# A hybrid attention layer: TensorE's order written out by hand through the attention, with the small steps spread over quarter granules

## The chip, the cores and the metric

One NeuronCore of a Trainium2 chip runs the whole layer. The metric is the device time of one execution in microseconds (us); the time before is the median of three runs.

## The reference, cut to what matters

One decoder layer for 512 tokens of width 2048, all in float32. Four heads of gated linear attention (GLA, in chunks) and four heads of differential softmax attention share one input projection; their outputs stand side by side and go through one output projection `w_o`.

```python
proj = h @ w_in                                   # 2048 -> 6160 columns
gq, gk, gv, gg, ga, dq, dk, dv = split(proj)
log_a = log_sigmoid(ga @ w_alpha_up + b_alpha) / 16
# GLA, per head (dk 128, dv 256):
#   o_t = q_t S_t,  S_t = diag(a_t) S_{t-1} + k_t^T v_t      (causal)
o_a = rmsnorm(gla(gq, gk, gv, log_a), gla_norm) * silu(gg)
# differential attention, per head and block of 128 queries:
#   p = softmax(q k^T * scale + alibi) for each of two halves;  a = p1 - lam * p2
o_b = rmsnorm(a @ dv, diff_norm) * (1 - lambda_init)
y = concat(o_a, o_b) @ w_o
```

Norms, the residual and a gated FFN with a short convolution follow; the change doesn't touch them.

## The kernel before, in words

**Products.** A float32 product is made of three TensorE matmuls on split numbers: high part times high part, and the two mixed ones. The left side stands in SBUF as `ah` and `al` (high and low parts of the activations, 16 slots of 128 features). The weights come in granules of 128x1024 (0.5 MB): SyncE (SP) issues a load into `raw` (4 buffers), ScalarE (ACT) writes the high part `whi` (L122), VectorE (DVE) the low part `wlo` (L123). A granule feeds 24 matmuls of 128x512, called products here.

**The attention stage.** From 395.86 us to about 670 us the kernel runs 31 granules (744 products): four each for `dq` and `dk` of diff head 3 (`stage_qk`, `proj_t`, `mm_t`, L158 to L160), eight for each of the two gate columns (`gate(0)`, `gate(1)`, `proj_n`, `mm_n`, L178 to L180), and the first seven of `w_o`'s first column. Everything before it made q, k, v and the decay sums of the heads and stored them in DRAM.

**The small work beside them.** Two generators hold the attention. `gla_chain` runs the four GLA heads one after the other: k·q (L745), seven levels of decayed scores (each four matmuls L736, with DVE and ACT work on the tiles `d` and `qe` and a masked copy into `sc`), then per head a serial tail: transposes of `kd` (L767), and for each of four chunks the output (L779, L780), its norm (ACT square, two POOL operations, DVE L784 into the SBUF tile `oa`), and the state (L787, DVE). `diff_chain` runs 16 blocks (4 heads, 4 query blocks): the scores of two halves (L813) with a softmax on DVE and ACT (L815 to L829, in `probs`), in the next step the transposes of the probabilities (L836, `turned`), in the one after the values (L844) with a norm, and last the transposes of the output (L855, `store`) to ACT and to DRAM (`dod`). `step()` runs once per granule and advances the two by GLA_PACE 2.0 and DIFF_PACE 0.7 steps.

**What sets the order.** The program only says which work belongs beside which granule. The Tile scheduler puts the instructions of each engine in order, TensorE's too, by a simulated time line; on the chip each engine then runs its list strictly in that order. PSUM has eight banks: four (`psm`) for the products' sums, four (`psa`) for all the small work, taken in turn. A tile with n buffers waits for the use n tiles back.

**The end of the stage.** `w_o` needs its left side in `ah` and `al`. The GLA part comes by `gla_rows` (load the gate `sg`, multiply `oa`, L929, transpose by L143 into slots 8 to 15), the diff part by `reload(h)` (load `dod` into `dr`, split into slots 2h and 2h+1). `FIRST` is the order of `w_o`'s granules; entry g takes slots 2g and 2g+1. Before, it begins with 4 and 5, the slots of GLA heads 0 and 1, which are ready only when their rows are transposed, in the middle of the small work; diff heads 0 and 1 (entries 0 and 1) follow.

Of the kernel before, what the change touches and what calls it, by code (L numbers as in the profile page):

```python
# [33 lines left out]
GLA_PACE, DIFF_PACE = 2.0, 0.7  # L34
# [3 lines left out]
def hybrid_layer(ctx: ExitStack, tc: tile.TileContext, x, attn_pre_norm, w_in, w_alpha_up, b_alpha,  # L38
# [10 lines left out]
    def dma(o, i):  # L49
        return nc.sync.dma_start(out=o, in_=i)  # L50

# [98 lines left out]
    def mm_t(banks, g, w, t0, t1, first=0, last=KT // 4 - 1):  # L150
# [12 lines left out]
    def proj_t(w3, col, emit, order=tuple(range(KT // 4))):  # L163
        banks = [bank(psm) for _ in range(2)]
        for g in order:
            w = granule(w3[:, 4 * g:4 * g + 4, col:col + 256], 4)
            mm_t(banks, g, w, 0, NT, order[0], order[-1])
            if g == order[-1]:
                for n in range(2):
                    emit(n, banks[n])  # L170
            step()
# [11 lines left out]
    def proj_n(w3, col, emit, order=tuple(range(KT)), first=0, banks=None, seq=tuple(range(KT // 2)), upto=KT // 2,  # L183
               after=None):
# [175 lines left out]
    dod = [dram.tile([P, 2, S], F32, name=f"dod{h}") for h in range(DH)]  # L360
    sgd = [dram.tile([P, NT, 512], F32, name=f"sgd{c}") for c in range(2)]
# [257 lines left out]
    def mix_unit(cols2, dsts, prods):  # L619
# [20 lines left out]
        def done(j):  # L640
            dma(dsts[j], st[j])
# [6 lines left out]
    units += [mix_unit((C_DQ + 256 * h, C_DK + 256 * h), (dqd[h], dkd[h]), up_prods) for h in range(STRASSEN_HEADS)]  # L648
# [40 lines left out]
    oa = [mc.tile([P, NT, 512], F32, name=f"oa{c}", bufs=1) for c in range(2)]  # L689
# [12 lines left out]
    SG = GDK ** -0.5  # L702

# [3 lines left out]
    def gla_head(h, q, k, b):  # L707
        bc = b.rearrange("p (c x) -> p c x", c=4)
        v = "p (n x) -> p n x"
        eb = mc.tile([P, S], F32, name="eb", tag="eb", bufs=1)  # L710
        sc = mc.tile([P, 4, P], F32, name="sc", tag="sc", bufs=1)
# [12 lines left out]
        def apply(hs, d):  # L724
# [4 lines left out]
            tt(d, d, k, ALU.mult)  # L729
# [20 lines left out]
        for li, hs in enumerate(LEVELS):  # L750
# [5 lines left out]
            if li + 2 == len(LEVELS):  # L756
                qb = tg("qb")
# [10 lines left out]
        kT = tg("kT")  # L768
        act(kT[:, :3 * P], kb[:, :3 * P], AF.Copy)
        yield  # L770
        vt = mc.tile([P, NT, GDV], F32, name="gv", tag="gv", bufs=1)
        dma(vt, gvd[h])
        g, e0 = h // 2, (h % 2) * GDV
        st = None
        for c in range(4):
# [8 lines left out]
            stt(oa[g][:, c, e0:e0 + GDV], po[:, :GDV], r, gnb, ALU.mult, ALU.mult)  # L784
# [9 lines left out]
            yield  # L794

# [67 lines left out]

    def gla_chain():
        nxt = gla_load(0)
        for h in range(GH):
            cur = nxt
            if h + 1 < GH:
                nxt = gla_load(h + 1)
            yield from gla_head(h, *cur)  # L870
            heads_done[0] = h + 1

    def diff_chain():
        todo = [(h, qb) for h in range(DH) for qb in range(NT)]
        held = [None] * 3
        while todo or any(held):
            for j, f in enumerate((store, values, turned)):
                if held[j]:
# [3 lines left out]
                    if j:  # L882
                        held[j - 1] = at, r
            if todo and todo[0][0] < heads_done[1]:
# [4 lines left out]
                if qb == NT - 1 and h + 1 < heads_done[1]:  # L889
# [3 lines left out]
    chains = [[gla_chain(), GLA_PACE, 0.0], [diff_chain(), DIFF_PACE, 0.0]]  # L893

    def both():
        while chains:
            for c in list(chains):
                c[2] += c[1]
                while c[2] >= 1.0:
                    c[2] -= 1.0  # L900
                    if next(c[0], 0) == 0:
                        chains.remove(c)
                        break
            yield

    def stage_qk(dsts, col, h, order=tuple(range(4))):
        def emit(n, b):
            t = mc.tile([P, S], F32, name="qs", tag="sg", bufs=2)
# [3 lines left out]
        proj_t(w_in3, col + 256 * h, emit, order)  # L912

    def gate(c):
        def emit(t, b):
            sg = mc.tile([P, S], F32, name="sg", tag="sg", bufs=2)
# [6 lines left out]
    def gla_rows(c, *ts):  # L923
        while heads_done[0] < 2 * c + 2:
            next(fill[0])
        for t in ts:
            sg = mc.tile([P, S], F32, name="sg", tag="sg", bufs=2)
# [12 lines left out]
    def reload(h):  # L940
        while heads_done[2] <= h:
            next(fill[0])
# [542 lines left out]
```

## Time and profile before

| | us |
|---|---|
| time, median of three runs | 2125.69 (2123.19 to 2129.04) |
| the profiled execution's own time | 2126.07 |
| its span in the profile | 2124.3 |
| TensorE busy in the span | 2074.1 (98%) |
| VectorE busy | 1559.1 (73%) |
| ScalarE busy | 960.4 (45%) |
| attention stage, 395.86 to 670 | 274.1, of which TensorE is busy 261.1 |

The profile tells for each engine when it was busy and, for each stretch of idle time, what ended it. TensorE's granted clock is given as a share of full speed: 1.00 is the upper of its two levels (2.4 GHz), a mean below it means that part of the stretch ran at the lower one (1.2 GHz).

### The profile page before, as it was taken

What the parts mean: (1) busy time and instruction counts of PE and PEld (TensorE: products, weight loads), DVE (VectorE), ACT (ScalarE), POOL (GpSimd) and SP (SyncE); (2) the same over time, 40 slices, a digit from 0 to 9 for tenths busy, and PEclk for the clock granted to TensorE, in tenths of its full rate; (3) what the DMA queues carried; (4) which work ended last, traced back from release to release, by engine and by line L of the source; (5) the groups of instructions that cost most, each with busy time, mean ns of one, the idle gap of its engine ahead of it and who ended that gap; (6) DMA issues with size and microseconds to landing.
All of it is one profiled execution on the core that took longest, in us unless ns stands there. A gap on an engine that the chain in (4) does not pass through costs nothing.

```text
span 2124.3 us, 34800 instructions
## 1 busy us (share of the span) xinstructions
PE 2074.1 (98%) x14161; PEld 1895.9 (89%) x14161; DVE 1559.1 (73%) x1873; ACT 960.4 (45%) x1217; POOL 245.4 (12%) x279
## 2 busy tenths in 40 slices
PE   7999999999989999999999999999999999999997
PEld 5899999888867888899999999999999888888886
DVE  7967667566785246788787786787878877988887
ACT  5435344345453234354544554544454554444433
POOL 1110111000011000011101111111111110110101
PEclk9999999999999999999999999999999999999999
DMA  7576675843425334465766757667577876776753
GB/s 263 140 173 168 152 179 134 287 127 126 134 83 186 99 129 169 129 139 129 171 168 159 175 135 192 149 157 192 132 171 174 249 215 176 181 198 156 182 155 139
DMA packets 251811, 349.10 MB, mean 164 GB/s; under 512 B 13744, under 2 KB 183140, under 8 KB 249860
## 3 DMA queue, kind: packets, MB, share of 16 engines
q1 hardware_dynamic: 181092, 265.09, 36.5%
q0 software_dynamic: 70560, 81.80, 24.6%
q8 instruction: 111, 1.82, 0.3%
q14 instruction: 48, 0.39, 0.1%
HBM read 301.23 MB, written 45.61 MB: 163 GB/s over the span
## 4 chain that ended last, share of the span: by engine, by line
PE 39%; issue 14%; DVE 3%; DMA 2%; POOL 1%; ACT 0%; POOLq 0%; DVEq 0%; SPq 0%; ACTq 0%
PE bank L316 11%; PE bank L315 11%; PE bank L314 11%; PE bank L160 1%; PE bank L159 1%; PE bank L158 1%; DVE wlo L123 1%; DMA raw<-in_w_ffn_out_dram 1%; POOL rt L228 1%; POOL raw L228 1%; PE bank L1266 1%; PE bank L1267 1%; DMA rt<-in_w_ffn_out_dram 0%; PE bank L1265 0%; PE bank L1390 0%
## 5 line engine op out<-in xcount | busy, mean ns | idle before, releaser
L122 ACT ACTIVATE whi<-raw 128x1024 fp32r<-128x1024 f32 x314 | 331.6, 1060 | 530.9 <-PE bank L315 164.1
L123 DVE TENSOR_TENSOR wlo<-raw,whi 128x1024 fp32r<-128x1024 f32 x314 | 381.6, 1221 | 242.9 <-ACT whi L122 236.7
L122 ACT ACTIVATE whi<-rt 128x1024 fp32r<-128x1024 f32 x306 | 322.8, 1060 | 357.3 <-PE bank L315 194.9
L123 DVE TENSOR_TENSOR wlo<-rt,whi 128x1024 fp32r<-128x1024 f32 x306 | 373.4, 1221 | 143.6 <-ACT whi L122 143.3
L314 PE MATMUL bank<-ah,whi 128*128 128x256 f32 x1600 | 442.3, 276 | 3.0 <-ACT gvs L528 2.1
L316 PE MATMUL bank<-ah,wlo 128*128 128x256 f32 x1600 | 442.4, 276 | 0.3 <-DVE wlo L123 0.2
L315 PE MATMUL bank<-al,whi 128*128 128x256 f32 x1600 | 442.0, 276 | 0.0
L314 PEld LDWEIGHTS bank<-ah,whi 128*128 128x128 f32 x1600 | 300.4, 188 | 3.9 <-ACT gvs L528 2.6
L316 PEld LDWEIGHTS bank<-ah,wlo 128*128 128x128 f32 x1600 | 300.3, 188 | 0.8 <-DVE wlo L123 0.7
L315 PEld LDWEIGHTS bank<-al,whi 128*128 128x128 f32 x1600 | 300.3, 188 | 0.1
L1266 PE MATMUL bank<-wlo,ah 128*128 128x512 f32 x560 | 219.0, 391 | 1.2 <-DVE wlo L123 1.2
L1267 PE MATMUL bank<-whi,al 128*128 128x512 f32 x560 | 218.5, 391 | 0.0
L1265 PE MATMUL bank<-whi,ah 128*128 128x512 f32 x560 | 213.6, 391 | 3.6 <-DVE acc L1273 1.9
L178 PE MATMUL bank<-whi,ah 128*128 128x512 f32 x448 | 177.6, 399 | 0.7 <-ACT ah L135 0.7
L179 PE MATMUL bank<-wlo,ah 128*128 128x512 f32 x448 | 177.6, 397 | 0.6 <-DVE wlo L123 0.6
L180 PE MATMUL bank<-whi,al 128*128 128x512 f32 x448 | 177.7, 400 | 0.0
L1265 PEld LDWEIGHTS bank<-whi,ah 128*128 128x128 f32 x560 | 105.2, 188 | 27.9 <-ACT whi L122 2.1
L1266 PEld LDWEIGHTS bank<-wlo,ah 128*128 128x128 f32 x560 | 105.5, 188 | 24.4 <-DVE wlo L123 2.5
L1267 PEld LDWEIGHTS bank<-whi,al 128*128 128x128 f32 x560 | 105.5, 188 | 21.9
L314 PE MATMUL bank<-s5h,whi 128*128 128x256 f32 x400 | 110.6, 276 | 1.0 <-ACT whi L122 1.0
L316 PE MATMUL bank<-s2h,wlo 128*128 128x256 f32 x400 | 110.8, 277 | 0.0
L316 PE MATMUL bank<-s5h,wlo 128*128 128x256 f32 x400 | 110.6, 276 | 0.0
(275 smaller groups left out, 4324.1 us busy)
## 6 DMA issues: line engine op xcount, KB each, us to landing
raw<-in_w_ffn_in_dram SPq DMA_DIRECT2D x96, 512.0 KB, 5.1
raw<-in_w_in_dram SPq DMA_DIRECT2D x64, 512.0 KB, 4.5
raw<-in_w_ffn_out_dram SPq DMA_DIRECT2D x48, 512.0 KB, 6.0
rt<-in_w_ffn_in_dram SPq DMA_DIRECT2D x40, 512.0 KB, 5.8
rt<-in_w_ffn_in_dram POOLq DMA_DIRECT2D x40, 512.0 KB, 5.9
raw<-in_w_ffn_in_dram POOLq DMA_DIRECT2D x40, 512.0 KB, 7.1
raw<-in_w_o_dram SPq DMA_DIRECT2D x32, 512.0 KB, 3.8
rt<-in_w_ffn_out_dram SPq DMA_DIRECT2D x20, 512.0 KB, 8.1
```

What stands on the lines that cost most here:

```text
L122: act(hi, raw, AF.Copy)
L123: tt(lo, raw, hi.bitcast(F32), ALU.subtract)
L178: mm(banks[t], ah[:, t, s, :], w[0][:, k, :], start=st, stop=False)
L179: mm(banks[t], ah[:, t, s, :], w[1][:, k, :], start=False, stop=False)
L180: mm(banks[t], al[:, t, s, :], w[0][:, k, :], start=False, stop=sp)
L228: nc.gpsimd.dma_start(out=raws[g].rearrange("p (a b) -> p a b", a=self.a), in_=self.block(0, j, g), accum_op=ALU.add)
L314: mm(o, wh, sh[:, :, kk, :], start=start and kk == 0 and n == 0, stop=False, **NOW)
L315: mm(o, wh, sl[:, :, kk, :], start=False, stop=False, **NOW)
L316: mm(o, wl, sh[:, :, kk, :], start=False, stop=kk == HK - 1, **NOW)
L1265: mm(b[j], sh[:, o:o + P], w[0][:, q, :], start=start and st == 0, stop=False, **NOW)
L1266: mm(b[j], sh[:, o:o + P], w[1][:, q, :], start=False, stop=False, **NOW)
L1267: mm(b[j], sl[:, o:o + P], w[0][:, q, :], start=False, stop=st == 3, **NOW)
```

## The change

- TensorE's order through the stage is the program's own (`manual_schedule` for that engine); the other engines are still ordered by the scheduler.
- `tick()` takes the place of `step()` there. It is called four times per granule, after every six products, and advances the GLA chain by 1.45/4 steps and the diff chain by 0.68/2 (a diff step now has two halves: store and values, then turned and scores). It also takes one entry of `turns`, the row work of `gla_rows`.
- `gla_head` ends after the levels; its serial tail is `gla_tail` and runs step by step beside the next head's levels. `eb` and `sc` have two buffers, `qb` and `kT` tiles of their own; `apply` multiplies only the first half of each pair in `d`, since the level reads no more.
- The GLA outputs no longer stay in `oa`: a tile `go` is stored to DRAM (`god`) from the POOL queue (`dma_aside`), and `gla_rows` loads it back into `ro` (two buffers) two rows ahead of its transposes.
- `gla_load(0)` and `diff_load(0)` stand ahead of the stage; the last two stores of diff head 2's q and k (`dqd`, `dkd`) go to the POOL queue.
- `FIRST` begins with 0, 1 (diff heads 0 and 1); `reload(0)` and `reload(1)` come after granules 5 and 6 of gate column 1, `gla_rows(0)` after its last, `gla_rows(1)` after `w_o`'s third. The order LATE moves from gate column 1 to gate column 0.

```diff
-GLA_PACE, DIFF_PACE = 2.0, 0.7
+GLA_PACE, DIFF_PACE = 1.45, 0.68
...
+    def dma_aside(o, i):
+        return nc.gpsimd.dma_start(out=o, in_=i)
...
+                if tick and k % 2:
+                    tick()
...
+                if tick:
+                    tick()
...
+    units += [mix_unit((C_DQ + 256 * h, C_DK + 256 * h), (dqd[h], dkd[h]), up_prods,
+                       dma_aside if h == STRASSEN_HEADS - 1 else dma) for h in range(STRASSEN_HEADS)]
...
-            tt(d, d, k, ALU.mult)
+            tt(dv[:, :, :hs], dv[:, :, :hs], k.rearrange(v, n=nb)[:, :, :hs], ALU.mult)
...
+        tails.append(gla_tail(h, kd, qb, eb, sc, vt))
+
+    def gla_tail(h, kd, qb, eb, sc, vt):
...
-            stt(oa[g][:, c, e0:e0 + GDV], po[:, :GDV], r, gnb, ALU.mult, ALU.mult)
+            go = mc.tile([P, GDV], F32, name="go", tag="go", bufs=2)
+            stt(go, po[:, :GDV], r, gnb, ALU.mult, ALU.mult)
+            dma_aside(god[h // 2][:, c, e0:e0 + GDV], go)
...
+    gla_in = {0: gla_load(0)}
+    diff_load(0)
+
     def gla_chain():
-        nxt = gla_load(0)
         for h in range(GH):
-            cur = nxt
             if h + 1 < GH:
-                nxt = gla_load(h + 1)
-            yield from gla_head(h, *cur)
-            heads_done[0] = h + 1
+                gla_in[h + 1] = gla_load(h + 1)
+            old = list(tails)
+            tails.clear()
+            for _ in gla_head(h, *gla_in[h]):
+                for g in old:
+                    next(g, None)
+                yield
+            for g in old:
+                for _ in g:
+                    yield
+        yield from tails[0]
...
+    chains = {"gla": [gla_chain(), GLA_PACE / 4, 0.0], "diff": [diff_chain(), DIFF_PACE / 2, -0.5]}
+
+    def advance(n):
+        if n in chains and next(chains[n][0], 0) == 0:
+            del chains[n]
+
+    def tick():
+        for n, c in list(chains.items()):
+            c[2] += c[1]
+            if c[2] >= 1.0:
+                c[2] -= 1.0
+                advance(n)
+        if turns:
+            turns.pop(0)()
+
+    turns = []
...
+    def gla_rows(c):
         while heads_done[0] < 2 * c + 2:
-            next(fill[0])
-        for t in ts:
-            sg = mc.tile([P, S], F32, name="sg", tag="sg", bufs=2)
+            advance("gla")
+        at = []
+
+        def fetch(t):
+            sg = mc.tile([P, S], F32, name="sg", tag="sg", bufs=3)
             dma(sg, sgd[c][:, t, :])
-            tt(oa[c][:, t, :], oa[c][:, t, :], sg, ALU.mult)
-            transpose_into_act(oa[c][:, t, :], t, 8 + 4 * c, 4)
-
-    fill.append(both())
-    pace[0], pace[1] = 1.0, 0.0
-    for h in range(STRASSEN_HEADS, DH):
-        late = (2, 3, 0, 1) if h == STRASSEN_HEADS else (0, 1, 2, 3)
-        stage_qk(dqd, C_DQ, h, late)
-        stage_qk(dkd, C_DK, h)
-        heads_done[1] = h + 1
+            o = mc.tile([P, S], F32, name="ro", tag="ro", bufs=2)
+            dma(o, god[c][:, t, :])
+            tt(o, o, sg, ALU.mult)
+            at.append(o)
+
+        def run(t):
+            if t > 1:
+                transpose_into_act(at[t - 2], t - 2, 8 + 4 * c, 4)
+            if t < NT:
+                fetch(t)
+
+        turns.extend(lambda t=t: run(t) for t in range(NT + 2))
...
     def after_gate(i):
-        if i in (4, 5):
-            gla_rows(0, 2 * (i - 4), 2 * (i - 4) + 1)
-        elif i > 5:
-            reload(i - 6)
+        if i in (5, 6):
+            reload(i - 5)
+        if i == 7:
+            gla_rows(0)
 
     def after_out(i):
         if i == 1:
             reload(2)
-        elif i in (2, 3):
-            gla_rows(1, 2 * (i - 2), 2 * (i - 2) + 1)
+        if i == 2:
+            gla_rows(1)
 
     LATE = (4, 5, 6, 7, 0, 1, 2, 3)
-    FIRST = (4, 5, 0, 1, 2, 6, 7, 3)
+    FIRST = (0, 1, 4, 5, 2, 6, 7, 3)
     order = [(s + 8) % 16 for s in range(KT)]
-    proj_n(w_in3, C_GG, gate(0))
-    proj_n(w_in3, C_GG + 512, gate(1), seq=LATE, after=after_gate)
-    banks = proj_n(w_o3, 0, None, order, seq=FIRST, upto=7, after=after_out)
-    drain()
+    with tc.manual_schedule(engines={ET.PE}):
+        for h in range(STRASSEN_HEADS, DH):
+            late = (2, 3, 0, 1) if h == STRASSEN_HEADS else (0, 1, 2, 3)
+            stage_qk(dqd, C_DQ, h, late)
+            stage_qk(dkd, C_DK, h)
+            heads_done[1] = h + 1
+        proj_n(w_in3, C_GG, gate(0), seq=LATE, tick=tick)
+        proj_n(w_in3, C_GG + 512, gate(1), after=after_gate, tick=tick)
+        banks = proj_n(w_o3, 0, None, order, seq=FIRST, upto=7, after=after_out, tick=tick)
+        while chains:
+            tick()
```

The order of instructions at three places. In these lists a row is one instruction or several alike in a row (x4), with the tile it writes and those it reads.

TensorE, the first granule of the stage (`dq`, L158 to L160; `gr` are the tiles that GLA head 0's q and k are loaded to). Before, the k·q matmuls stand behind 65 products of the stage:

```order
L158 MATMUL bank<-ah,whi 128x512
L159 MATMUL bank<-al,whi 128x512
L745 MATMUL bank<-gr 128x128 x4
L160 MATMUL bank<-ah,wlo 128x512
L158 MATMUL bank<-ah,whi 128x512
```

After, the same matmuls (now L753, the products L161 to L163) stand behind 18:

```order
L162 MATMUL bank<-al,whi 128x512
L163 MATMUL bank<-ah,wlo 128x512
L753 MATMUL bank<-gr 128x128 x4
L161 MATMUL bank<-ah,whi 128x512
L162 MATMUL bank<-al,whi 128x512
```

The first use of GLA head 0's tiles has moved 47 products ahead.

TensorE, between the end of gate column 1 and the first product of `w_o`, before: the beginning of a run of small rows with no product among them.

```order
L836 MATMUL bank<-ident,s 128x128 x2
L813 MATMUL bank<-dr 128x384 x2
L736 MATMUL bank<-qe,d 128x64 x8
L767 MATMUL bank<-ident,kd 128x128 x3
L780 MATMUL bank<-gv,sc 128x256
L787 MATMUL bank<-gv,kT 128x256
L855 MATMUL bank<-ident,on 128x128 x2
L844 MATMUL bank<-dv,aT 128x256 x2
L836 MATMUL bank<-ident,s 128x128 x3
L813 MATMUL bank<-dr 128x512 x2
L779 MATMUL bank<-st,qb 128x256
L780 MATMUL bank<-gv,sc 128x256
```

After, the densest place of the whole stage, beside the levels of head 1 (L744 level, L790, L791 and L800 a tail step, L850 transposed probabilities, L827 scores):

```order
L162 MATMUL bank<-al,whi 128x512
L163 MATMUL bank<-ah,wlo 128x512
L744 MATMUL bank<-qe,d 128x64 x4
L790 MATMUL bank<-st,qb 128x256
L791 MATMUL bank<-gv,sc 128x256
L800 MATMUL bank<-gv,kT 128x256
L850 MATMUL bank<-ident,s 128x128 x4
L827 MATMUL bank<-dr 128x128 x2
L161 MATMUL bank<-ah,whi 128x512
```

The run of small rows is gone; the densest place has six rows between two products.

SP's queue where `gla_rows(1)` works. Before, rows need only the gate (`sg`), loaded behind the stores of diff blocks (`dod`):

```order
L50 DMA dr<-dod_107 128x512 x2
L50 DMA dod_108<-do 256x1x128
L50 DMA raw<-in_w_o_dram 128x2x512 x4
L50 DMA sg<-sgd_110 128x512
L50 DMA dod_108<-do 256x1x128
L50 DMA raw<-in_w_o_dram 128x2x512
L50 DMA sg<-sgd_110 128x512
```

After, each row also needs its `ro`, and a load of `ro` waits for the buffer that the transposes two rows back release:

```order
L50 DMA ro<-god_110 128x512
L50 DMA sg<-sgd_112 128x512
L50 DMA ro<-god_110 128x512
L50 DMA sg<-sgd_112 128x512
L50 DMA dod_108<-do 256x1x128
L50 DMA raw<-in_w_o_dram 128x2x512 x2
L50 DMA ro<-god_110 128x512
L50 DMA dod_108<-do 256x1x128
```

Eight loads have been added to this queue over the two calls of `gla_rows`, with weight loads (`raw`) queued among them.

## Rows read from the trace of the kernel before

**Rows 1.** The page: busy time of each engine, share of the span, instructions.

```profile
PE 2074.1 (98%) x14161; PEld 1895.9 (89%) x14161; DVE 1559.1 (73%) x1873; ACT 960.4 (45%) x1217; POOL 245.4 (12%) x279
```

**Rows 2.** Stretches: us, busy time of five engines, TensorE's clock, DMA share, GB/s.

```profile
395.86:520.00 124.14, 124.14 (x626) 104.20 (x625) 79.03 (x183) 54.90 (x103) 7.49 (x18) 1.00 0.52 179
...
580.00:590.00 10.00, 5.42 (x32) 4.35 (x31) 7.72 (x19) 6.58 (x11) 0.00 (x0) 0.96 0.66 210
590.00:600.00 10.00, 8.47 (x32) 5.78 (x31) 8.33 (x21) 4.76 (x15) 2.41 (x6) 0.86 0.54 171
600.00:610.00 10.00, 6.11 (x32) 5.25 (x30) 7.38 (x25) 6.10 (x19) 2.68 (x6) 0.83 0.14 44
...
sum 274.14, PE 261.12 PEld 216.03 DVE 188.61 ACT 124.26 POOL 28.06; mean PE 37.30 PEld 30.86 DVE 26.94 ACT 17.75 POOL 4.01
```

**Rows 3.** TensorE's waits, 395.86 to 674: waiter, releaser, us total, times, longest.

```profile
PE bank L780 <- DVE nm L819: 4.6, 1, 4.6
PE bank L836 <- DVE s L829: 4.1, 2, 3.9
PE bank L779 <- DVE st L792: 2.6, 2, 1.3
```

**Rows 4.** TensorE's time line, 583 to 610: start, us, line, [idle before, releaser].

```profile
589.49 1.22 PE L780 MATMUL bank<-gv,sc 128*128 128x256 f32 x2 [4.58 <-DVE nm L819]
...
598.90 0.59 PE L780 MATMUL bank<-gv,sc 128*128 128x256 f32 x2
...
605.34 0.66 PE L836 MATMUL bank<-ident,s 128*128 128x128 f32 x4 [3.89 <-DVE s L829]
...
607.89 1.92 PE L745 MATMUL bank<-gr 128*128 128x128 f32 x8
```

**Rows 5.** TensorE's time line, 399 to 412.

```profile
399.97 0.39 PE L158 MATMUL bank<-ah,whi 128*128 128x512 f32 x1
...
410.62 1.05 PE L745 MATMUL bank<-gr 128*128 128x128 f32 x8
```

**Rows 6.** SP's DMA issues in time, 398 to 400.

```profile
398.30 0.37 SPq L50 DMA_DIRECT2D raw<-in_w_in_dram  x1
...
399.42 0.52 SPq L50 DMA_DIRECT2D gr<-gkd  x1
```

**Rows 7.** DMA issues, 388 to 412: count, KB each, median us to landing.

```profile
raw<-in_w_in_dram SPq DMA_DIRECT2D x3, 512.0 KB, 9.3
...
gr<-gkd SPq DMA_DIRECT2D x2, 256.0 KB, 7.8
```

**Rows 8.** VectorE's time line at 407.7.

```profile
407.73 0.43 DVE L719 TENSOR_TENSOR d<-gr 128x256 f32<-128x256 f32 x1 [4.11 <-DMA gr<-bd]
```

**Rows 9.** TensorE's time line at 502: a level between products.

```profile
501.78 1.00 PE L736 MATMUL bank<-qe,d 128*128 128x64 f32 x8
502.59 0.48 PE L180 MATMUL bank<-whi,al 128*128 128x512 f32 x1
```

**Rows 10.** TensorE's time line: outputs of two GLA chunks.

```profile
518.13 0.59 PE L780 MATMUL bank<-gv,sc 128*128 128x256 f32 x2
...
537.75 0.59 PE L780 MATMUL bank<-gv,sc 128*128 128x256 f32 x2
```

**Rows 11.** VectorE's time line: the same two outputs, normed.

```profile
524.75 0.47 DVE L784 SCALAR_TENSOR_TENSOR oa<-bank,rs,gnb 128x256 f32<-128x256 f32 x1
...
540.22 0.48 DVE L784 SCALAR_TENSOR_TENSOR oa<-bank,rs,gnb 128x256 f32<-128x256 f32 x1
```

**Rows 12.** DMA issues, 592 to 680.

```profile
dr<-dod SPq DMA_DIRECT2D x8, 256.0 KB, 3.1
```

**Rows 13.** Duration of a DMA issue on POOL, ns: lowest, median, highest.

```profile
L683 POOL DMA_DIRECT2D al<-a21l x1: 733/733/733, 389.7 to 389.7; - x1
```

**Rows 14.** Groups by shape, 410 to 680: busy us, mean ns, idle before.

```profile
L929 DVE TENSOR_TENSOR oa<-oa,sg 128x512 f32<-128x512 f32 x8 | 5.5, 693 | 1.6 <-DMA sg<-sgd 1.4
...
L828 DVE TENSOR_SCALAR s<-s,r 128x512 f32<-128x512 f32 x4 | 1.9, 482 | 0.0
```

More of the change, by code (lines that the diff above doesn't have):

```diff
@@ L148, in bcast_row, with mm_t @@
         dma(tile_ap, row.partition_broadcast(P))
-    def mm_t(banks, g, w, t0, t1, first=0, last=KT // 4 - 1):
+    def mm_t(banks, g, w, t0, t1, first=0, last=KT // 4 - 1, tick=None):
         for n in range(2):
@@ L160, in mm_t, with proj_t @@
                 mm(o, wl, ah[:, t0:t1, kk, :], start=False, stop=sp)
-    def proj_t(w3, col, emit, order=tuple(range(KT // 4))):
+                if tick and k % 2:
+                    tick()
+    def proj_t(w3, col, emit, order=tuple(range(KT // 4)), tick=None):
         banks = [bank(psm) for _ in range(2)]
@@ L166, in proj_t @@
             w = granule(w3[:, 4 * g:4 * g + 4, col:col + 256], 4)
-            mm_t(banks, g, w, 0, NT, order[0], order[-1])
+            mm_t(banks, g, w, 0, NT, order[0], order[-1], tick)
             if g == order[-1]:
@@ L170, in proj_t @@
                     emit(n, banks[n])
-            step()
     def mm_n(banks, t, g, w, first=None, last=None):
@@ L183, in proj_n @@
     def proj_n(w3, col, emit, order=tuple(range(KT)), first=0, banks=None, seq=tuple(range(KT // 2)), upto=KT // 2,
-               after=None):
+               after=None, tick=None):
         if banks is None:
@@ L360, in hybrid_layer @@
     dod = [dram.tile([P, 2, S], F32, name=f"dod{h}") for h in range(DH)]
+    god = [dram.tile([P, NT, 512], F32, name=f"god{c}") for c in range(2)]
     sgd = [dram.tile([P, NT, 512], F32, name=f"sgd{c}") for c in range(2)]
@@ L617, in mixer_sums, with mix_unit @@
             yield
-    def mix_unit(cols2, dsts, prods):
+    def mix_unit(cols2, dsts, prods, store=dma):
         st = {}
@@ L640, in done @@
         def done(j):
-            dma(dsts[j], st[j])
+            store(dsts[j], st[j])
         return Unit(4, block, prods, seven, quarters(quad, copy, done))
@@ L688, in hybrid_layer @@
     mc = mixer.enter_context(tc.tile_pool(name="mc", bufs=2, reuse_waits="tile"))
-    oa = [mc.tile([P, NT, 512], F32, name=f"oa{c}", bufs=1) for c in range(2)]
     def tg(name):
@@ L702, in hybrid_layer @@
     SG = GDK ** -0.5
+    tails = []
     def gla_load(h):
@@ L794, in gla_head @@
             yield
+        heads_done[0] = h + 1
     SC = DQK ** -0.5
@@ L883, in diff_chain @@
                         held[j - 1] = at, r
+                if j == 1:
+                    yield
             if todo and todo[0][0] < heads_done[1]:
@@ L888, in diff_chain @@
                 held[2] = (h, qb), probs(h, qb)
-                if qb == NT - 1 and h + 1 < heads_done[1]:
+                if qb == NT - 2 and h + 1 < heads_done[1]:
                     diff_load(h + 1)
             yield
[L893 to L904, printed above, removed]
+    chains = {"gla": [gla_chain(), GLA_PACE / 4, 0.0], "diff": [diff_chain(), DIFF_PACE / 2, -0.5]}
[11 more added lines that the diff above has]
+    turns = []
     def stage_qk(dsts, col, h, order=tuple(range(4))):
         def emit(n, b):
-            t = mc.tile([P, S], F32, name="qs", tag="sg", bufs=2)
+            t = mc.tile([P, S], F32, name="qs", tag="sg", bufs=3)
             act(t, b, AF.Copy)
             dma(dsts[h][:, n, :], t)
-        proj_t(w_in3, col + 256 * h, emit, order)
+        proj_t(w_in3, col + 256 * h, emit, order, tick)
     def gate(c):
         def emit(t, b):
-            sg = mc.tile([P, S], F32, name="sg", tag="sg", bufs=2)
+            sg = mc.tile([P, S], F32, name="sg", tag="sg", bufs=3)
             act(sg, b, AF.Sigmoid)
@@ L921, in gate @@
         return emit
-    def gla_rows(c, *ts):
+    def gla_rows(c):
         while heads_done[0] < 2 * c + 2:
-            next(fill[0])
-        for t in ts:
-            sg = mc.tile([P, S], F32, name="sg", tag="sg", bufs=2)
+            advance("gla")
+        at = []
+        def fetch(t):
+            sg = mc.tile([P, S], F32, name="sg", tag="sg", bufs=3)
             dma(sg, sgd[c][:, t, :])
-            tt(oa[c][:, t, :], oa[c][:, t, :], sg, ALU.mult)
-            transpose_into_act(oa[c][:, t, :], t, 8 + 4 * c, 4)
-    fill.append(both())
-    pace[0], pace[1] = 1.0, 0.0
-    for h in range(STRASSEN_HEADS, DH):
-        late = (2, 3, 0, 1) if h == STRASSEN_HEADS else (0, 1, 2, 3)
-        stage_qk(dqd, C_DQ, h, late)
-        stage_qk(dkd, C_DK, h)
-        heads_done[1] = h + 1
+            o = mc.tile([P, S], F32, name="ro", tag="ro", bufs=2)
[8 more added lines that the diff above has]
+        turns.extend(lambda t=t: run(t) for t in range(NT + 2))
     def reload(h):
         while heads_done[2] <= h:
-            next(fill[0])
+            advance("diff")
         for n in range(2):
```

15 lines of the change are left out of this document (7 added, 8 removed).

## Prediction

> **What bounds the kernel now.** I read the page's busy line first: TensorE is busy for 98% of the span, so the change can only win back what TensorE loses [rows 1]. The view by stretches, taken over the attention stage, shows where that is. From 395.86 to 520 us TensorE has no idle time at all. Of the whole 274.14 us it is busy for 261.12, and most of the 13.0 us of idle time stand between 580 and 610 (4.58, 1.53 and 3.89 us), where its mean granted clock is 0.96, 0.86 and 0.83 as well [rows 2]. The view of waits names the enders: the output step of a GLA chunk (L780) waits 4.6 us, the transposes of the probabilities (L836) 3.9 us, a state (L779) 1.3 us, all for VectorE [rows 3]. The time line of TensorE shows the price of the clock too. Behind the wait of 4.58 us L780 takes 1.22 us, and 0.59 where nothing was waited for; behind the wait of 3.89 us the four k·q matmuls (L745) take 1.92 [rows 4], against 1.05 in the first head [rows 5]. So the matmuls behind the two long waits go at about half speed: these two rows lose 0.63 and 0.87 us, five others beside them (states, values, outputs) 1.8, in all 3.3; the clock column says much the same (0.4 + 1.4 + 1.7 = 3.5 us over three stretches of ten).
>
> The reason is the order. Between the end of gate column 1 and 614 us no product stands in TensorE's list, because `w_o` begins with the slots of GLA heads 0 and 1, whose rows are not there yet. About 29 rows of small work stand in one heap. In it two softmax blocks ask VectorE for more time between scores and transposes than TensorE has work between them (10.5 against 4.7 us, and 8.4 against 5.2), and TensorE waits for the difference.
>
> **The change part by part.**
>
> *The heap goes.* The steps are spread by 6 products, and `w_o` begins with diff heads 0 and 1, which are stored long before. I went through the 16 blocks of the new order: between scores (L827) and transposes (L850) TensorE has at least 4.6 us more work than VectorE in each, so none of them waits. Won: the idle 13.0 us and the 3.3 us of slow matmuls, 16.3 by these rows. Measured from start to start, less the usual pitch, the seven waits cost 14.7 instead of 13.0, since a matmul's modelled end overlaps its successor; that gives 18.0. I take **-18.0** and keep 16.3 for the range.
>
> *The same matmuls finely spread.* Their number does not change. Eight records of a level (L736) between products take 0.81 us from the first's start to the next product's, 0.10 us each with the switch in it [rows 9], so being spread adds nothing to see. Cost: 0. Half of `d` is multiplied no more, which takes work from VectorE, busy 188.61 of 274.14 us [rows 2], and not from the path: 0.
>
> *A new wait at the start.* The k·q of head 0 (L753) now stands behind 18 products of the stage instead of 65. TensorE starts the nineteenth product of the stage at 399.97 [rows 5], so that is when it is there now. The tiles' loads stand in SP's queue behind a weight load issued at 398.30, which waits for a buffer that the change does not free earlier; the later of the two that k·q needs, `gkd`, is issued at 399.42 [rows 6] and takes 7.8 us [rows 7], to 407.2. The third load, `bd`, lands half a microsecond later: VectorE's first use of it starts at 407.73 behind a wait of 4.11 us [rows 8]. TensorE now waits for `gkd`, in order, with all products of the stage behind it. Bounds: a load of the same 256 KB takes 3.1 us when little else runs [rows 12], which would leave 2.6 us; the 9.3 us of the weight loads [rows 7] would make it 8.8. The row itself says 7.2. The last two stores (0.5 MB each) leave SP's queue and may spare the loads up to 1.3 us of shared transfer time (0.5 MB at the 390 GB/s moved there), giving 5.9. I take **+6.5**, nearest the load's own row, and behind so long a wait the lower clock as in [rows 4]: **+1.7**. Level 0 of head 0 follows 18 products later (4.1 us), and VectorE and ScalarE need some 4.9 us from the landing of `bd` to its tiles, of which the products and k·q cover nearly all: 0.
>
> Beside this row the Trainium skill (DMA: Bandwidth & Descriptors, "Issuing engines are not separate DMA queues") says that DMAs started from different engines run on the same 16 DMA engines, and that starting them elsewhere saves only issue time. By it the two stores moved to POOL would spare the loads nothing, the wait would be 7.2, and the sum 0.7 higher; no row of before tells the two apart.
>
> *Rows of the GLA heads through DRAM.* `ro` has two buffers, so the load of row t+2 is issued behind the transposes of row t. A load (3.1 us [rows 12]) and the multiplication (0.69 us [rows 14]) make 3.8, and TensorE has 3.2 to 4.6 us of work in between. `sg` of the next row, and in the second call weight loads, stand in the same queue. Four rows in each call, two of them short: I take 1.0 for heads 0 and 1, 1.4 for heads 2 and 3, **+2.4** (1 to 4).
>
> *Banks of the small work.* All small work shares four PSUM banks in turn, and in the new order two places use six of them without a product between (level, tail step, transposes, scores). There the second scores need the bank that the tail step's output has. Such a bank is free when VectorE has read the normed output (L784): in an ordinary case 2.4 us from the end of L780 to the end of L784 (538.34 to 540.70), in the slowest 6.5 (518.72 to 525.22) [rows 10, 11]; most of the 16 lie between 2.0 and 2.8. TensorE has 1.2 us of other work there: 1.1 each, 2.2 for both. The store of each output (`god`) is issued on POOL ahead of the next norm's two POOL operations; an issue there takes 0.73 us [rows 13], some 0.8 in the two places. Together **+3.0** (1 to 9).
>
> The Trainium skill (SBUF — State Buffer, the note on the "DVE blocks DMA" trap) says that a DMA issued from POOL can't get its descriptors written while VectorE runs certain two-port operations. By it a store could wait for one such operation, 0.48 us for a scaling of the probabilities [rows 14], in the two dense places: the sum would be 1 us higher. No run here shows it yet.
>
> *Boundaries of the gate columns* (four banks emptied at once) and the middle of the stage: 0 to 1, I take 0, since before has no idle time there [rows 2].
>
> **Sum**, against the profiled execution's own 2126.07: 2126.07 - 18.0 + 6.5 + 1.7 + 2.4 + 3.0 = 2121.7. That execution lies 0.4 above the median, so 2121.3.
>
> **The rivals.**
>
> A, much faster: the start costs little. The scheduler's new order and the empty SP queue let the loads go early, the wait is the 2.6 us of an undisturbed load, the clock stays. 2126.07 - 18.0 + 2.6 + 2.4 + 3.0 = 2116.1, or 2117.8 with the lower reading of the gain. For it: `gla_load(0)` stands first in the program. Against: the weight load at 398.30 is still ahead of it in the queue, and the queue is kept in order.
>
> B, slower: the outputs' banks come free late everywhere. The norm runs over ScalarE, POOL and VectorE, and each is ordered by the scheduler, not by the new hand-written order; if a store's issue or other POOL and VectorE work keeps the bank for 6.5 us as in the slowest row [rows 10, 11], 14 places of the new order use the bank too soon, and the shortfalls sum to 28.3 us in place of 3.0. With 8.2 for the start and 2.4 for the rows: 2126.07 - 18.0 + 8.2 + 2.4 + 28.3 = 2147. At 4.3 us it is only six places and 8.8 us (2127). It ends above 2132 from about 4.8 us on. For it: a POOL queue with 16 stores more. Against: 2.0 to 2.8 us in nearly all rows of before, under a busier VectorE.
>
> C, no gain: the waits move. What VectorE cannot do in time in the heap it cannot do elsewhere, and new waits of the same total arise (2126). Against it: VectorE is busy for 69% of the stage [rows 2], so it has the time once the work is spread.
>
> **How the numbers follow.** Forecast case 0.58 (2117 to 2127), A 0.18, B 0.16, C 0.08. About 0.3% (6.4 us) can be told from no change here: faster is below 2119.3, slower above 2132.1. Faster: A and 0.22 of the forecast case, 0.40. Slower: B, 0.16. Within: the other 0.36 of the forecast case and C, 0.44. The range takes A's times (2114 to 2118) and ends at 2131, which leaves out B and a little below A, under 0.2.
>
> **What would show it.** In the profile after: no TensorE wait above 1 us for the softmax (L843) or the masked copy, and a clock of 1.00 at the end of the stage, show the first term right. One wait of 6 to 7 us at L753 near 400 us, ended by a DMA to `gr`, shows the second; if it is under 3 us, A holds. Waits at L146 for `ro` of 1 us or less show the third, waits at L827 ended by L796 the fourth; ten of these or more mean B. I would be wrong altogether if waits stood in the gate columns' middle, at the levels (L744).

## The result, and the profile after

The changed kernel takes 2148.35 us (median of four runs, 2146.37 to 2155.3) against 2125.6 before: a ratio of 1.0112, 95% interval 1.0084 to 1.0139. It is slower by over 20 us where 4 us less were forecast; its profiled execution (2146.62 us) lies 24.9 above the sum of the prediction.

The page of the changed kernel, the line that answers to [rows 1]: TensorE is busy 7 us longer, and the span grew from 2124.3 to 2144.9 us.

```profile
PE 2081.1 (97%) x14161; PEld 1901.4 (89%) x14161; DVE 1553.2 (72%) x1873; ACT 960.9 (45%) x1217; POOL 260.1 (12%) x297
```

To see where, it helps to cut the run at lines that both kernels have. One matmul of the transposed products (L158 before, L161 after) starts the attention stage and also runs in the first two column pairs of the FFN; the FFN's last part begins with L1265 (L1305 after). The view of one line gives the first and last start. Before:

```profile
L158 PE MATMUL bank<-ah,whi x256: 276/377/478, 395.9 to 912.5; 128*128 128x512 f32 x64, 128*128 128x256 f32 x64
L1265 PE MATMUL bank<-whi,ah x560: 387/389/628, 1670.4 to 2069.7; 128*128 128x512 f32 x187
```

After:

```profile
L161 PE MATMUL bank<-ah,whi x256: 276/377/799, 395.5 to 922.5; 128*128 128x512 f32 x64, 128*128 128x256 f32 x64
L1305 PE MATMUL bank<-whi,ah x560: 389/389/502, 1691.6 to 2090.0; 128*128 128x512 f32 x187
```

From the stage's first product to the last of the first pairs: 516.6 us before, 527.0 after, 10.4 more. From there to L1305: 757.9 before, 769.1 after, **11.2 more, in a part of the program that the change was not meant to touch.** What comes behind differs by 0.6.

TensorE's waits from 390 to 700 us, after (answers to [rows 3]; waiter, releaser, total us, times, longest):

```profile
PE bank L753 <- DMA gr<-gkd: 6.6, 1, 6.6
PE bank L146 <- DVE ro L962: 6.2, 4, 3.2
PE bank L827 <- DVE on L863: 2.2, 1, 2.2
PE bank L146 <- DVE al L139: 1.3, 1, 1.3
```

The waits of the heap are gone; those at L753 (k·q of the first head) and L146 (transposes of the rows) are new. TensorE's time line, after (answers to [rows 4, 5]):

```profile
406.32 2.05 PE L753 MATMUL bank<-gr 128*128 128x128 f32 x8 [6.58 <-DMA gr<-gkd]
...
553.60 0.88 PE L827 MATMUL bank<-dr 128*128 128x384 f32 x2 [2.16 <-DVE on L863]
...
647.67 1.08 PE L146 MATMUL bank<-ident,ro 128*128 128x128 f32 x4 [3.17 <-DVE ro L962]
648.40 0.77 PE L182 MATMUL bank<-whi,ah 128*128 128x512 f32 x1
648.98 0.63 PE L183 MATMUL bank<-wlo,ah 128*128 128x512 f32 x1
649.40 0.63 PE L184 MATMUL bank<-whi,al 128*128 128x512 f32 x1
```

Behind the waits of 6.58, 2.16 and 3.17 us a product follows the other after 0.43 us, where 0.23 is usual. The stretches of ten us around them (answers to [rows 2]; the column that matters is the third from the right, the granted clock):

```profile
405.00:415.00 10.00, 8.68 (x36) 7.52 (x37) 7.43 (x18) 4.85 (x7) 0.00 (x0) 0.70 1.05 407
...
550.00:560.00 10.00, 7.84 (x36) 6.07 (x35) 7.83 (x18) 5.84 (x13) 0.86 (x2) 0.83 0.34 93
...
640.00:650.00 10.00, 5.23 (x24) 4.01 (x24) 5.45 (x9) 1.79 (x3) 0.61 (x1) 0.83 0.55 184
650.00:660.00 10.00, 10.00 (x40) 8.14 (x39) 3.23 (x5) 2.39 (x6) 2.09 (x5) 0.83 0.34 103
```

A mean of 0.70 over ten us says that 6 of them ran at the lower level (1.2 GHz). Not all of that is lost, since part of it lies in the wait itself. What it costs is read from the starts: behind the first wait the k·q matmuls take 1.70 us to the next product (0.81 in the kernel before, 410.62 to 411.43), and the next seven products 3.09 (to 411.11) instead of some 1.7, **2.3 us** together. In the same way the clock costs some 2.9 us behind the wait of 3.17 at the rows, and some 1.7 behind the wait of 2.16 at L827, where the whole low stretch lies behind the wait.

And the FFN's beginning (waits of TensorE from 910 to 1710 us, after):

```profile
PE bank L322 <- DVE wlo L126: 4.2, 3, 2.0
PE bank L320 <- ACT s3h L138: 1.4, 1, 1.4
PE bank L320 <- ACT whi L125: 1.0, 1, 1.0
```

These waits all lie between 934 and 950 us, and around them the clock is lower too (0.95 over 100 us, before 1.00):

```profile
900.00:1000.00 100.00, 93.32 (x672) 88.25 (x671) 84.75 (x84) 45.47 (x50) 10.31 (x8) 0.95 0.47 105
```

Before, the profile shows no wait of TensorE between 912 and 1670 us. `s2h`, `s3h` and their low parts are split sums of the FFN's left side. VectorE's view of the low parts, before (first and last start behind the durations) and then after:

```profile
L136 DVE TENSOR_TENSOR s5l<-u,s5h x2: 1217/1218/1218, 872.0 to 903.4; 128x1024 fp32r<-128x1024 f32 x2
L136 DVE TENSOR_TENSOR s3l<-u,s3h x2: 1216/1221/1226, 885.1 to 923.4; 128x1024 fp32r<-128x1024 f32 x2
```

```profile
L139 DVE TENSOR_TENSOR s5l<-u,s5h x2: 1215/1216/1216, 917.6 to 919.8; 128x1024 fp32r<-128x1024 f32 x2
L139 DVE TENSOR_TENSOR s3l<-u,s3h x2: 1211/1212/1212, 949.5 to 950.6; 128x1024 fp32r<-128x1024 f32 x2
```

Before, the two halves of each sum are some 30 us apart, the first half beside the FFN's second pair of columns. After, both halves stand back to back, at the end of that pair and behind it. The reason is one line of the diff: `proj_t` lost its call of `step()`. In the attention `tick()` replaces it. But the FFN's first pairs call `proj_t` too, without a tick, and there `step()` was what advanced `up_sums`, the generator of these sums, by one part per granule. Now `drain()` does all of it at the end.

### The profile page after: what moved, and what is told of

It reads as the page before. It is cut to its first block, busy times and chain, and to the rows that moved or that the text cites. A ratio compares the mean times of both kernels' runs of the same rounds, so it can differ in the third digit from the quotient of the medians.

```text
span 2144.9 us, 34818 instructions
## 1 busy us (share of the span) xinstructions
PE 2081.1 (97%) x14161; PEld 1901.4 (89%) x14161; DVE 1553.2 (72%) x1873; ACT 960.9 (45%) x1217; POOL 260.1 (12%) x297
## 3 DMA queue, kind: packets, MB, share of 16 engines
q8 instruction: 111, 1.82, 0.3%
## 4 chain that ended last, share of the span: by engine, by line
PE 29%; issue 24%; DVE 3%; POOL 2%; DMA 2%; ACT 0%; POOLq 0%; DVEq 0%; ACTq 0%
PE bank L322 8%; PE bank L321 8%; PE bank L320 8%; PE bank L163 1%; PE bank L161 1%; PE bank L162 1%; DVE wlo L126 1%; POOL rt L234 1%; POOL raw L234 1%; DMA raw<-in_w_ffn_out_dram 1%; PE bank L1430 0%; PE bank L1431 0%; PE bank L1429 0%; DMA raw<-in_w_ffn_in_dram 0%; DVE u L1463 0%
## 5 line engine op out<-in xcount | busy, mean ns | idle before, releaser
L1305 PE MATMUL bank<-whi,ah 128*128 128x512 f32 x560 | 213.1, 390 | 4.5 <-DVE acc L1313 1.8
L182 PE MATMUL bank<-whi,ah 128*128 128x512 f32 x448 | 185.6, 416 | 0.1
L1305 PEld LDWEIGHTS bank<-whi,ah 128*128 128x128 f32 x560 | 104.9, 188 | 28.8 <-ACT whi L125 3.9
L320 PE MATMUL bank<-s3h,whi 128*128 128x256 f32 x400 | 110.8, 277 | 1.4 <-ACT s3h L138 1.4
```

The source lines that it names most:

```text
L182: mm(banks[t], ah[:, t, s, :], w[0][:, k, :], start=st, stop=False)
L320: mm(o, wh, sh[:, :, kk, :], start=start and kk == 0 and n == 0, stop=False, **NOW)
L1305: mm(b[j], sh[:, o:o + P], w[0][:, q, :], start=start and st == 0, stop=False, **NOW)
```

## The experiments

Each ratio is to the kernel before, run beside it on the same chip. "Stage" is the distance used above, from the first to the last start of that one matmul line, in the profiled execution; "FFN" the distance from there to the start of the FFN's last part. Each distance is that of one execution. Kernels with the same program in the stage differ in it by 1.5 us (before and e2_before_no_step) and 1.2 us (after and e1_step), so a difference of a microsecond or two says nothing.

| kernel | ratio to before, 95% interval | stage, us | FFN, us |
|---|---|---|---|
| before | 1 | 516.6 | 757.9 |
| after | 1.0112 (1.0084 to 1.0139) | 527.0 | 769.1 |
| e1_step | 1.0060 (1.0038 to 1.0082) | 528.2 | 758.5 |
| e2_before_no_step | 1.0053 (1.0038 to 1.0068) | 518.1 | 770.4 |
| e3_late | 1.0007 (0.9996 to 1.0019) | 518.0 | 761.3 |
| e4_rows | 1.0037 (1.0019 to 1.0055) | 523.0 | 758.6 |
| e5_both | 0.9942 (0.9925 to 0.9958) | 502.9 | 760.6 |
| e6_auto | 0.9958 (0.9941 to 0.9975) | 508.0 | 758.7 |
| e8_first | 0.9984 (0.9970 to 0.9999) | 513.0 | 758.9 |
| e9_both_auto | 0.9935 (0.9912 to 0.9958) | 501.0 | 758.9 |
| e10_early | 1.0023 (1.0006 to 1.0040) | 521.8 | 760.0 |

**e1_step: the lost line, put back.**

```diff
             if g == order[-1]:
                 for n in range(2):
                     emit(n, banks[n])
+            if tick is None:
+                step()
```

> The changed kernel with one line put back: the call of step() at the end of each granule in proj_t, where no tick is given, which is the FFN's first pair of granules only. Theory (the sums for the FFN's split products are no longer spread over its granules and pile up on VectorE and ScalarE): the waits of TensorE between 930 and 950 us (0.4, 1.9, 1.0, 1.4, 2.0) and the lower clock there (0.95 over 100 us) go, and the time falls by 9 to 12 us from the changed kernel's 2146 to 2150, to about 2137. Rival (the waits there come from a shifted order of transfers or buffers, an echo of the attention stage): the time stays within 3 us of the changed kernel.

Measured: the ratio falls from 1.0112 to 1.0060, about 11 us; the FFN part is 758.5 us as before, and TensorE has no wait left from 900 to 1100 us. The stage is unchanged. The theory holds.

**e2_before_no_step: the same line taken from the kernel before.**

```diff
-            step()
+            if go:
+                step()
...
-        proj_t(w_in3, col + 256 * h, emit, order)
+        proj_t(w_in3, col + 256 * h, emit, order, go=True)
```

> The kernel before with only the call of step() in proj_t taken out where the FFN uses it; the attention keeps it. Theory: 9 to 12 us slower than before (about 2136), with TensorE's waits for s2l, s3h and the weights' low parts at the FFN's start as in the changed kernel. Rival: within 3 us of before.

Measured: 1.0053, some 11 us slower, with the FFN part at 770.4 us. TensorE's waits from 900 to 1100 us are those of the changed kernel:

```profile
PE bank L317 <- DVE wlo L123: 3.8, 2, 1.9
PE bank L315 <- ACT s3h L135: 1.4, 1, 1.4
PE bank L315 <- ACT whi L122: 1.0, 1, 1.0
```

So the line alone, without anything in the attention, makes this loss.

**e3_late: e1_step with the GLA chain begun later.**

```diff
-    chains = {"gla": [gla_chain(), GLA_PACE / 4, 0.0], "diff": [diff_chain(), DIFF_PACE / 2, -0.5]}
+    chains = {"gla": [gla_chain(), GLA_PACE / 4, -2.6], "diff": [diff_chain(), DIFF_PACE / 2, -0.5]}
```

> As e1_step, and the GLA chain begins 2.6 steps later, so that the first k·q (L753 in the changed kernel) stands behind 60 products of the stage and no longer behind 18. Theory (the wait of 6.6 us for gkd and the lower clock behind it, 0.70 over ten us, cost about 10 us): 9 to 11 us less than e1_step, about 2127, with no wait at the first k·q. Rival (the loads are late whatever stands before them, and the next matmul that needs them waits as long): less than 4 us won, with a wait at level 0 (L744) or at the first scores instead.

Measured: 1.0007 against 1.0060, 11 us, and 10.2 us of stage. But two other waits stand in its place, on TensorE's time line:

```profile
410.31 1.41 PE L829 MATMUL bank<-dr 128*128 128x128 f32 x4 [3.72 <-DMA dr<-dkd]
...
650.85 1.04 PE L792 MATMUL bank<-st,qb 128*128 128x256 f32 x2 [3.88 <-DVE st L807]
```

The first scores now come before their tiles have landed (the rival, in part), which the wait at k·q had hidden. And the GLA chain, 2.6 steps late, isn't done when `gla_rows(1)` is called; its last tail step is then run at once, six products behind the one before it, and waits for that one's state.

**e4_rows: e1_step with the rows spread over more ticks.** `gla_rows(0)` is called one granule earlier, and its work takes the ticks of a plan in place of one each.

```diff
-        turns.extend(lambda t=t: run(t) for t in range(NT + 2))
+        turns.extend((lambda t=t: run(t)) if t is not None else (lambda: None) for t in PLAN[c])
...
+    PLAN = ((0, 1, None, None, 2, None, 3, None, 4, None, 5), (0, 1, None, 2, 3, None, 4, 5))
...
-        if i == 7:
+        if i == 6:
             gla_rows(0)
```

> As e1_step, and the rows of the GLA heads are spread over more ticks: gla_rows(0) is called one granule earlier and its loads and transposes lie over 11 ticks in place of 6, those of gla_rows(1) over 8. Buffers stay two. Theory (the chain load, multiply, transposes of two buffers is longer than the products between, and costs 7.5 us of waits at the transposes and some 3.4 of lower clock at 640 to 660): 7 to 11 us less than e1_step, about 2128, waits at the transposes under 1.5 us in all. Rival (the waits there belong to VectorE and SP's queue being late for other work): less than 4 us won.

Measured: 1.0037 against 1.0060, which their intervals don't separate; the stage is 5.2 us shorter. The waits for `ro` are gone and the clock is 1.00 from 600 to 650, but the time of others in the same place has grown:

```profile
PE bank L802 <- ACT aT L854: 2.2, 1, 2.2
PE bank L829 <- DVE on L865: 2.2, 1, 2.2
PE bank L146 <- ACT whi L125: 2.0, 1, 2.0
PE bank L792 <- DVE st L807: 1.9, 1, 1.9
```

Half the expected gain, then. The chain through DRAM was one cause of the loss at 630 to 675; that the other is the in-order list meeting VectorE and ScalarE at the wrong moment is my reading of these enders, and no run isolates it.

**e5_both: e4_rows with both chains begun later.** The GLA chain is also made a little faster, so that it still ends in time.

```diff
-GLA_PACE, DIFF_PACE = 1.45, 0.68
+GLA_PACE, DIFF_PACE = 1.55, 0.68
...
-    chains = {"gla": [gla_chain(), GLA_PACE / 4, 0.0], "diff": [diff_chain(), DIFF_PACE / 2, -0.5]}
+    chains = {"gla": [gla_chain(), GLA_PACE / 4, -2.4], "diff": [diff_chain(), DIFF_PACE / 2, -1.5]}
```

> As e4_rows (step() back, rows over more ticks), with both chains begun later: the first k·q behind 54 products, the first scores behind 66, and GLA_PACE 1.55 so that the chain still ends before gla_rows(1). Theory (the start costs about 10 us: the tiles of the GLA chain land near 406.5, those of the diff chain near 410.3, and whatever is in TensorE's order ahead of that waits; the rest of the small waits is about 6): no wait above 1 us before 450, idle time of the stage 5 to 8 us, 10 to 14 us less than e1_step, 3 to 8 us faster than before. Rival (waits only move to the next in-order place): within 4 us of before or slower.

Measured: 0.9942, 12 us faster than before; the stage is 502.9 us. In it TensorE's waits come to 3.0 us, and the clock is 1.00 in every stretch:

```profile
PE bank L792 <- DVE st L807: 1.1, 1, 1.1
PE bank L852 <- DVE s L845: 1.0, 1, 1.0
PE bank L802 <- ACT aT L854: 0.9, 1, 0.9
```

More was won than the start could give: 20.1 us of stage from e4_rows, of which the start accounts for half.

**e6_auto and e9_both_auto: e1_step and e5_both without the hand-written order.**

```diff
-    with tc.manual_schedule(engines={ET.PE}):
+    if True:
```

> As e1_step, with TensorE's order left to the scheduler again; its list then has the first k·q behind 65 products and never more than 7 small rows without a product. Theory (the heap is gone by the paces and by w_o's new first granules, and it is the hand-written order alone that brings the waits at the start and for the rows): 8 to 14 us less than e1_step, at or below before. Rival (the hand-written order is what keeps TensorE fed, and the scheduler's order waits for VectorE as in the heap of before): as slow as e1_step or slower, with waits above 3 us at the transposes or outputs after 500.

> As e5_both, with TensorE's order left to the scheduler. Theory (once the chains begin late and the rows have time, the order written out by hand adds little: the scheduler's list of the same program has no heap either): within 5 us of e5_both, about 2115 to 2121, no wait above 3 us in the attention. Rival (the hand-written order is worth having by itself): 6 us or more slower than e5_both, with a wait of 4 us or so at the transposes of the probabilities as in e6_auto.

Measured: e6_auto is at 0.9958, 20.2 us of stage below e1_step where 8 to 14 were expected, with one wait above 1.5 us (4.17 us at 625.95 for the softmax). e9_both_auto is at 0.9935, the same as e5_both within the intervals, and in its stage TensorE hardly waits at all (stretches from 395 to 700 us, the sum):

```profile
sum 305.00, PE 304.45 PEld 253.26 DVE 199.78 ACT 137.58 POOL 40.77; mean PE 50.74 PEld 42.21 DVE 33.30 ACT 22.93 POOL 6.79
```

The scheduler puts the first k·q behind 65 products again, as before, where its tiles are there. The gain therefore comes from the new program (quarter granules, paces, tails beside the next head's levels, another first granule for `w_o`); which of its parts bring it, the runs don't separate, but for the first granule (e8_first). With the changed kernel's start and rows the hand-written order cost 20 us of stage (e1_step against e6_auto); with the late start and the spread rows it costs nothing that can be told (e5_both against e9_both_auto).

**e8_first: the kernel before with `w_o` beginning with diff heads 0 and 1.**

```diff
-    FIRST = (4, 5, 0, 1, 2, 6, 7, 3)
+    FIRST = (0, 1, 4, 5, 2, 6, 7, 3)
```

> The kernel before with one line changed: w_o begins with the slots of diff heads 0 and 1 (FIRST = 0, 1, 4, 5, ...). Theory of the prediction (the heap stands there because w_o's first granules need the rows of GLA heads 0 and 1): products move into the heap, the two waits of 4.6 and 3.9 us go, 8 to 16 us faster than before. Rival (the rows of diff heads 0 and 1 come as late: their loads into dr are issued at 594.93, when head 2's last scores have freed the buffers): within 4 us of before, the heap stays.

Measured: 0.9984, 3.6 us of stage. The wait at the outputs stays, and where the second one was, the first product of `w_o` now waits for the diff heads' own rows:

```profile
591.73 1.22 PE L780 MATMUL bank<-gv,sc 128*128 128x256 f32 x2 [4.50 <-DVE nm L819]
...
600.49 0.50 PE L178 MATMUL bank<-whi,ah 128*128 128x512 f32 x1 [1.19 <-ACT ah L135]
```

Those rows (`reload`) are loaded into `dr` buffers that head 2's last scores free: in the kernel before the loads are issued at 594.93 us, just behind these scores at 593.87. The rival holds mostly; the first granules of `w_o` explain the second long wait of the heap, not the first.

**e10_early: e5_both with the old start.**

```diff
-    chains = {"gla": [gla_chain(), GLA_PACE / 4, -2.4], "diff": [diff_chain(), DIFF_PACE / 2, -1.5]}
+    chains = {"gla": [gla_chain(), GLA_PACE / 4, 0.0], "diff": [diff_chain(), DIFF_PACE / 2, -0.5]}
```

> As e5_both, with the chains begun where the changed kernel begins them (first k·q behind 18 products); paces and rows as in e5_both. Theory (the start alone costs 6.6 to 7 us of wait and 3 to 5 us of lower clock behind it): 9 to 12 us slower than e5_both in the stage, the wait for gkd being the only one above 1.5 us. Rival (half of what e5_both won came from other phases of the steps, not from the start): 15 to 20 us slower, with waits at scores and transposes as in e4_rows.

Measured: 1.0023 against 0.9942, 17 us; the stage is 18.9 us longer. On TensorE's time line:

```profile
408.07 2.05 PE L755 MATMUL bank<-gr 128*128 128x128 f32 x8 [8.02 <-DMA gr<-gkd]
...
555.80 0.41 PE L852 MATMUL bank<-ident,s 128*128 128x128 f32 x2 [2.40 <-DVE s L845]
...
668.28 1.09 PE L146 MATMUL bank<-ident,ro 128*128 128x128 f32 x4 [4.58 <-DVE ro L964]
```

The start costs 8.0 us of wait and some 1.7 of lower clock behind it (1.70 us for the k·q matmuls, then four products in 1.82), 9.7, about half of the 18.9. The rest is what the rival said: the moment at which the later steps fall has changed with the start, and they wait where e5_both doesn't.

## Why the prediction was wrong, step by step

Going by the profiled executions, the terms of the sum and what each measured:

| step of the prediction | forecast, us | measured, us | from |
|---|---|---|---|
| the heap goes | -18.0 | -16.2 | e9_both_auto: 15.6 us of stage, 0.6 of wait left |
| a new wait at the start, clock behind it | +8.2 | +8.9 | 6.6 of wait, 2.3 of clock |
| rows through DRAM | +2.4 | +10.4 | 7.5 of wait at L146, 2.9 of clock |
| banks and other small waits | +3.0 | +6.7 | 5.0 of wait, 1.7 of clock behind L827 |
| outside the stage | 0 | +11.2 | L1305; e1_step, e2_before_no_step |

The first row is the least certain: e9_both_auto differs from the changed kernel in more than the heap. The measured column sums to +21.0; stage and FFN together differ by 21.6 (10.4 and 11.2), so 0.6 stays unplaced. The executions differ by 20.55, since the changed kernel is 0.4 us shorter ahead of the stage and 0.6 behind the FFN.

**The step that failed most was never written.** The prediction worked through the attention stage and set everything outside it to zero. The diff shows `-            step()` in `proj_t`; I read it as the move from `step()` to `tick()` and didn't ask who else calls `proj_t`. The text of the front part says that "`tick()` takes the place of `step()` there", which is true of the stage alone, and that the change doesn't touch the FFN, which it does. This is 11.2 of the 24.9 us, shown from both sides by e1_step and e2_before_no_step.

**The rows through DRAM** were rightly seen as a chain of load, multiplication and transposes longer than the products beside it, and wrongly sized. I took 3.8 us a row against 3.2 to 4.6 of cover. VectorE's time line of the changed kernel shows two of the rows:

```profile
641.21 0.69 DVE L962 TENSOR_TENSOR ro<-ro,sg 128x512 f32<-128x512 f32 x1 [2.48 <-DMA ro<-god]
...
646.83 0.69 DVE L962 TENSOR_TENSOR ro<-ro,sg 128x512 f32<-128x512 f32 x1 [2.41 <-DMA ro<-god]
```

and a load of `ro` takes 3.9 us here, not the 3.1 of [rows 12]. The multiplications end 5.6 us apart. SP's time line shows why, with its wait from 637 to 643 us below it:

```profile
637.09 0.55 SPq L50 DMA_DIRECT2D ro<-god  x1
641.93 0.32 SPq L50 DMA_DIRECT2D sg<-sgd  x1
642.35 0.37 SPq L50 DMA_DIRECT2D ro<-god  x1
```

```profile
SPq L50 <- DVE ro L962: 4.2, 1, 4.2
```

The next row's `ro` (642.35) stands in the queue behind a load of `sg` for a later row, and that load waits 4.2 us for one of the three buffers of `sg`: it is issued as the first row's multiplication ends (641.21 + 0.69). So the second buffer of `ro` wins nothing here. Multiplication, issue and load follow each other, 5.6 us for the row. The upper bound of 4 us was too low too: the clock behind the wait was not in it.

**The wait at the start** is the step that held: 6.58 us where 6.5 stood, ended by the DMA to `gr` as said. That it fits to 0.1 us is in part luck, since 6.5 was picked between 5.9 and 7.2. `gkd` is issued at 399.01 and TensorE goes on at 406.32, 7.3 us where 7.8 stood in [rows 7]. The Trainium skill's sentence that DMAs from different engines share the same engines (DMA: Bandwidth & Descriptors, "Issuing engines are not separate DMA queues") fits in the main: the two stores moved to POOL's queue brought the loads 0.5 us at most, of the 1.3 that I had allowed. The clock behind it was a little too small, 1.7 for 2.3.

**Rival B named the right time for the wrong reason.** It forecast 2147, by banks of the GLA outputs that come free late in 14 places. None of TensorE's long waits is ended by L796, the step that it named. One bank did come free late, that of a diff block's values: L858 writes it at 545.01, and L863 reads it last at 552.98. In between ScalarE, in order, works through this (time line of ScalarE, after):

```profile
547.05 1.04 ACT L125 ACTIVATE whi<-raw 128x1024 fp32r<-128x1024 f32 x1
548.11 1.28 ACT L946 ACT_TABLE_LOAD   x1
549.41 0.60 ACT L946 ACTIVATE sg<-bank 128x512 f32<-128x512 f32 x1
549.90 0.38 ACT L871 ACTIVATE do<-bank 128x256 f32<-128x256 f32 x1
550.16 0.39 ACT L860 ACTIVATE bank<-bank 128x256 f32<-128x256 f32 x1
```

The norm's square (L860) stands behind the first gate column's sigmoid with its table load. Behind it a third table load (550.68) holds ScalarE's L729 to 552.60, VectorE waits for that, and L863 comes next in its order:

```profile
552.63 0.43 DVE L737 TENSOR_TENSOR d<-d,gr 128x256 f32<-128x256 f32 x1 [1.03 <-ACT d L729]
552.98 0.48 DVE L863 SCALAR_TENSOR_TENSOR on<-bank,rs,dnb 128x256 f32<-128x256 f32 x1
```

That is a boundary of the gate columns, which the prediction had set to 0 to 1; it cost 2.2 us of wait at L827 and the clock behind it. A store's issue on POOL (0.61 us) plays no part in it. The Trainium skill's rule that a DMA issued from POOL can be held up by VectorE (SBUF — State Buffer, the note on the "DVE blocks DMA" trap) shows nowhere here: `god` lands 3.2 us (median) after its issue, and no wait of TensorE is put down to such a store.

**Rivals A and C.** A's short wait of 2.6 us at the start did not occur. C said that waits of the same total would come elsewhere, for want of VectorE time; e9_both_auto has the same VectorE work and 0.6 us of waits, so time on VectorE was not what lacked.

**The heap.** Its price came out at 16.2 us, near the lower of the two readings given (16.3, by idle time and clock); the one that I took, from start to start, is 1.8 higher, little more than two executions of one stage differ by. Its cause as told was right in small part only: e8_first, which changes what `w_o` begins with, removes 3.6 us of it. The rest went with the other parts of the new program, and no run says with which.

## What to carry to other kernels

A line removed from a shared helper acts at every call of the helper: before the stage in question is costed, list the callers, and look for whoever lived on a side effect of it (here a generator advanced by `step()`). An order written out by hand puts every wait of a small step in front of all the work behind it; give each such step a distance from its loads that the trace covers, at the start above all, look in the queue for loads that stand behind one that waits for a buffer, and compare with the scheduler's order of the same program, which here was as good as the best hand-written one (e9_both_auto beside e5_both) and without the late start still faster than before (e6_auto). Moving the start of a chain moves all its later steps against the engines they need, so two runs that differ in the start alone differ elsewhere also.

## What was not expected of the hardware

A wait of 3.17 us in front of products was followed by the lower clock for some 5 us (0.43 us from product to product up to 651, the upper level again at 653.5), and so was one of only 2.16 us at L827 (clock 0.83 from 550 to 560). The length of the wait alone doesn't decide it: in e4_rows the same matmul waits the same 2.16 us at 555.83, and the clock stays at 1.00 from 550 to 570.

```profile
550.00:560.00 10.00, 7.84 (x42) 6.16 (x41) 8.97 (x21) 7.23 (x12) 0.86 (x2) 1.00 0.34 93
```

The waits of 1.0 to 1.6 us in the attention stage of the changed kernel show no slow products behind them. So a wait for a row cost up to nearly twice its length (3.17 us and 2.9 more), which the prediction's bounds for single waits didn't hold.
